# Softmax weights divided by their row sums on GpSimd, before their transposes

## The chip, the cores and the metric

The kernel runs on one core of a Trainium2 chip. The metric is the device time of one execution in microseconds (us). TensorE is called PE here (its weight loads PEld), VectorE DVE, ScalarE ACT, GpSimd POOL, and SyncE, which issues the DMAs, SP.

## The reference

Two layers of a hybrid decoder, 512 tokens of width 1024, each with five attention branches of four heads of 64, which are gated, projected and summed. The change concerns how a softmax branch divides by its sums:

```python
def _masked_softmax(logits, mask):
    l = jnp.where(mask, logits, -jnp.inf)
    m = jnp.max(l, axis=-1, keepdims=True)
    ...
    e = jnp.where(mask, jnp.exp(l - m), 0.0)
    return e / jnp.maximum(jnp.sum(e, axis=-1, keepdims=True), 1e-30)
```

A is DSA (a top-k mask from an indexer), B is FoX (a forget-gate bias), D is NSA (a sum of a compressed, a selected and a window part, each with a gate per head and token), E is attention into 256 memory tokens. C, stick breaking, has no softmax. Each branch output is multiplied with SiLU of its `z` projection before it is projected to width 1024.

## The kernel before

Activations lie transposed, channels on the partitions and 512 tokens along the row. Weights come in tiles of 128x1024 (`wload`, L281): each is split by ACT and DVE (L269, L270) into a high part `whi` and a rest `wlo`, so that a projection (`proj`, L503) is 3 x 8 matmuls of 128x512 into one PSUM bank `pj`.

An attention section is a Python generator, and `weave` (L652) interleaves its steps with those of generators that project: mem attention with `merge(2)`, the NSA projections and top-k (L1392); NSA attention with `merge(4)`, `dsa_proj` and the rest of top-k (L1393); DSA attention with `merge(3)` and `fox_proj` (L1394); FoX attention with `merge(0)` (L1395); then `merge(1, YB)` alone (L1396). `merge` needs the finished branch (`yhi`, `ylo`) that it projects. The tile framework sets the order of each engine at build time: it takes instructions in order of emission as far as their inputs and buffers are ready by its own cost estimates, weight loads earlier (`early`, L291). `after` (L191) pins a few orders by hand. At run time each engine keeps the order that it was given.

`causal` (L572) handles a causal softmax branch by blocks of 128 queries, i = 0 to 3, each with 128(i+1) keys, one head per step. A head: `qk` writes scores to a bank of tag `S` (two banks); `softmax_p` (L542) adds the mask and takes the row extreme on DVE (tile `P`, `nm`), then ACT takes the exponential with the sum of each row to `sums`. `finish`, called two heads later (lag 2), transposes `P` by 128x128 pieces on PE into a bank of tag `T` (three banks, tile `pt`), and evacuates it to `PT` on ACT or DVE in turn. After the fourth head `pv_pair` (L562) multiplies values with `PT` into a bank `Y` (channels on partitions, 128 queries along the row), and `done` follows. `P` has three buffers, shared by tag with two other tiles.

Queries lie along the row of `Y`, so the sums, one per query on its partition, do not fit it. `head_rows` (L611) takes the reciprocals `r` (`inv_sums`, L605), spreads each over 64 columns (`rb_`; on ACT at L616, or on DVE at L618 with the NSA gate), and transposes that in two pieces on PE (L621) into a bank `hr`. `gated_y` (L637) multiplies `hr` with `Z` to `g` (L640), then `Y` with `g` (L642), and `finish_y` splits `y` into `yhi` and `ylo`. NSA (L1180) does so for each of its two causal parts: `hr` copied to `rs_` (L1183), `Y` times `rs_` to `od` (L1185); the compressed part comes from two matmuls into a third bank `oc`; two adds (L1193, L1194) and the product with `Z` (L1196) end the block. `mem_attn` (L1259) works by pairs of heads, without a lag, its four heads of a block in one `Y`.

POOL only fills halves of key tiles with zeros (`k_stack`, L476).

## Time and profile before

| | |
|---|---|
| median of 3 runs | 1350.59 us (1350.27 to 1351.06) |
| the profiled execution, its own time | 1351.01 us |
| its span | 1349.2 us |
| PE busy | 1310.1 us (97%), 7240 matmuls |
| DVE busy | 892.8 us (66%) |
| ACT busy | 689.0 us (51%) |
| POOL busy | 11.4 us (1%) |

The span runs from the first to the last instruction that was recorded; the time of the execution has some 1.8 us more around it. Durations below are from that one execution. Recorded times of PE's neighbouring matmuls overlap, so where one ends against the next tells more than its duration. Waits are inferred from semaphores, and a wait is put down to what came last.

### The profile page before, as it was taken

How to read it: one execution, taken by the hardware profiler on the slowest of the kernel's cores; microseconds unless marked ns; L12 is line 12 of the kernel's file. 1: busy time of each engine (PE TensorE's matmuls, PEld its weight loads, DVE VectorE, ACT ScalarE, POOL GpSimd, SP SyncE). 2: the span in 40 equal slices, each digit the busy share in tenths (PEclk: the TensorE clock that was granted, in tenths of full speed). 3: DMA queues.
4: the chain of work that ended last, by engine and by line, in shares of the span. 5: the costliest groups of instructions: out<-in, count | busy, mean ns of one | idle time of the engine just before them, and what ended most of it. 6: DMA issues, size and time to landing. Idle time of an engine off the chain costs nothing.

```text
span 1349.2 us, 18962 instructions
## 1 busy us (share of the span) xinstructions
PE 1310.1 (97%) x7240; PEld 1068.4 (79%) x7240; DVE 892.8 (66%) x1847; ACT 689.0 (51%) x1300; POOL 11.4 (1%) x28
## 2 busy tenths in 40 slices
PE   7999999999999999999999999999999999999997
PEld 6777777878888788878887777777788778887896
DVE  6887999767655444545567799995676463454554
ACT  6887834357545434434447795534574452343340
POOL 0000000000000000000000000000000000000000
PEclk9999999999999999999999999999999999999998
DMA  6442321321123132224524313222122222323231
GB/s 215 139 127 77 110 78 63 94 78 59 63 79 102 55 94 78 71 84 130 183 81 126 109 63 110 85 68 84 57 69 63 86 86 66 100 77 103 94 111 63
DMA packets 40235, 124.11 MB, mean 92 GB/s; under 512 B 4432, under 2 KB 6480, under 8 KB 40144
## 3 DMA queue, kind: packets, MB, share of 16 engines
q1 hardware_dynamic: 40144, 122.89, 28.5%
q8 instruction: 57, 0.93, 0.3%
q14 instruction: 34, 0.28, 0.1%
HBM read 118.16 MB, written 4.72 MB: 91 GB/s over the span
## 4 chain that ended last, share of the span: by engine, by line
PE 70%; ACT 6%; DVE 5%; issue 2%; DVEq 0%; ACTq 0%
PE pj L259 58%; PE Y L259 3%; PE S L259 3%; PE pt L556 3%; ACT whi L269 2%; DVE wlo L270 1%; PE hr L621 1%; ACT sw L430 1%; ACT sw L431 1%; PE sbz L259 1%; DVE P L546 0%; ACT P L547 0%; DVE score L902 0%; DVE m L901 0%; ACT Qi L848 0%
## 5 line engine op out<-in xcount | busy, mean ns | idle before, releaser
L259 PE MATMUL pj<-h_hi,whi 128*128 128x512 f32 x1088 | 429.5, 396 | 0.7 <-DVE rt L433 0.7
L259 PE MATMUL pj<-h_hi,wlo 128*128 128x512 f32 x1088 | 429.0, 394 | 0.0
L259 PE MATMUL pj<-h_lo,whi 128*128 128x512 f32 x1088 | 429.0, 394 | 0.0
L270 DVE TENSOR_TENSOR wlo<-wraw,whi 128x1024 fp32r<-128x1024 f32 x183 | 223.7, 1223 | 228.1 <-ACT whi L269 217.0
L269 ACT ACTIVATE whi<-wraw 128x1024 fp32r<-128x1024 f32 x183 | 193.4, 1058 | 319.9 <-PE pj L259 213.9
L259 PEld LDWEIGHTS pj<-h_hi,wlo 128*128 128x128 f32 x1088 | 204.5, 188 | 42.8 <-DVE wlo L270 2.3
L259 PEld LDWEIGHTS pj<-h_hi,whi 128*128 128x128 f32 x1088 | 204.6, 188 | 40.5 <-issue 1.7
L259 PEld LDWEIGHTS pj<-h_lo,whi 128*128 128x128 f32 x1088 | 204.6, 188 | 40.4 <-issue 1.8
L547 ACT ACTIVATE P<-P,nm 128x128 f32<-128x128 f32 (+3 forms) x128 | 71.6, 559 | 67.7 <-DVE nm L546 64.2
L259 PE MATMUL pj<-yhi,whi 128*128 128x512 f32 (+1 forms) x192 | 71.9, 374 | 2.9 <-ACT yhi L269 2.9
L259 PE MATMUL pj<-yhi,wlo 128*128 128x512 f32 (+1 forms) x192 | 71.6, 373 | 0.0
L259 PE MATMUL pj<-ylo,whi 128*128 128x512 f32 (+1 forms) x192 | 71.5, 372 | 0.0
L556 PE MATMUL pt<-CA,P 128*128 128x128 f32 x384 | 62.7, 277 | 2.6 <-ACT P L1274 1.3
L546 DVE CUSTOM_DVE_ANT_0 P<-S,CA 128x128 f32<-128x128 f32 (+3 forms) x104 | 47.6, 468 | 18.1 <-PE S L259 18.0
L556 PEld LDWEIGHTS pt<-CA,P 128*128 128x128 f32 x384 | 44.9, 141 | 18.2 <-ACT P L1274 6.0
L259 PE MATMUL S<-Ks,Qs 128*128 128x256 f32 (+2 forms) x160 | 51.0, 358 | 6.6 <-DVE nm L546 6.5
L394 ACT ACTIVATE G<-pj 128x512 f32<-128x512 f32 x92 | 53.6, 582 | 0.3
L902 DVE MATCH_REPLACE8 score<-m,score 128x256 f32<-128x256 f32 (+2 forms) x96 | 51.7, 541 | 0.0
L901 DVE MAX8 m<-score 128x8 f32<-128x256 f32 (+2 forms) x96 | 49.7, 546 | 0.0
L799 DVE SCALAR_TENSOR_TENSOR G<-G,pj 128x512 f32<-128x512 f32 x64 | 43.6, 681 | 3.6 <-PE pj L259 3.3
L800 DVE TENSOR_TENSOR acc<-acc,G 128x512 f32<-128x512 f32 x64 | 44.0, 688 | 0.9
L259 PEld LDWEIGHTS pj<-yhi,whi 128*128 128x128 f32 x192 | 36.2, 188 | 10.4 <-ACT yhi L269 4.0
(478 smaller groups left out, 2006.1 us busy)
## 6 DMA issues: line engine op xcount, KB each, us to landing
wraw<-in_wall_dram SPq DMA_DIRECT2D x192, 512.0 KB, 3.7
wc<-in_wall_dram SPq DMA_DIRECT2D x16, 256.0 KB, 6.1
x<-in_xt_dram SPq DMA_DIRECT2D x8, 256.0 KB, 7.0
mraw<-in_memt_dram SPq DMA_DIRECT2D x4, 512.0 KB, 4.7
xo<-in_xt_dram SPq DMA_DIRECT2D x8, 256.0 KB, 4.3
xspill<-xn SPq DMA_DIRECT2D x8, 256.0 KB, 2.2
xo<-xspill SPq DMA_DIRECT2D x8, 256.0 KB, 4.0
out_dram<-o SPq DMA_DIRECT2D x8, 256.0 KB, 2.2
```

The source lines that it names most:

```text
L259: return nc.tensor.matmul(out_, lhsT, rhs, start=start, stop=stop, **kw)
L269: nc.scalar.activation(hi, raw, AF.Copy)
L270: nc.vector.tensor_sub(lo, raw, hi.bitcast(F32))
L394: i = nc.scalar.activation(*a, **k)
L430: nc.scalar.activation(sw[a], p[b], AF.Copy)
L546: nc.vector.tensor_tensor_reduce(P, S, mask, -1.0, 3e38, OP.add, OP.min, nm)
L547: nc.scalar.activation(P, P, AF.Exp, bias=nm, scale=-1.0, accum_out=sums)
L556: nc.tensor.transpose(pt[:, 128 * j:128 * j + 128], x[:, c:c + 128], ident)
L799: nc.vector.scalar_tensor_tensor(G, G, gc, p, op0=gop, op1=OP.mult)
L800: nc.vector.tensor_add(acc, acc, G)
L901: nc.vector.max(m8, lv.work[i])
L902: nc.vector.match_replace(lv.work[i], m8, lv.work[i], REPL)
```

## The change

After each second head of a part (in mem attention: after each pair), `inv_sums` is taken of the two heads' sums, in NSA multiplied with the two gates, and GpSimd multiplies each of the two `P` tiles, in place, with its column of it. The transposes then take the divided weights, so `head_rows` goes, with `hr`, `rb_`, `rs_`, `g` and `od`. In NSA the selected part, the window part and the compressed part (`rest`) all add up in one bank `Y`; the first matmul alone starts it. `gated_y` multiplies `Y` with `Z` directly. The lag of `causal` goes from two heads to three, mem attention gets a lag of one pair, and the tag of `P` has five buffers in place of three. `hold` keeps what `after_qk` did: a PV group comes after the scores issued last. In the diff, blank lines and longer runs of removed lines are left out (the functions before stand above):

```diff
@@ -541,7 +541,7 @@
     def softmax_p(S, n, mask, sums):
-        P = wk.tile([128, T], F32, name="P", tag="P", bufs=3)[:, :n]
+        P = wk.tile([128, T], F32, name="P", tag="P", bufs=5)[:, :n]
         nm = sm.tile([128, 1], F32, name="nm", bufs=6)
         nc.vector.tensor_tensor_reduce(P, S, mask, -1.0, 3e38, OP.add, OP.min, nm)
         nc.scalar.activation(P, P, AF.Exp, bias=nm, scale=-1.0, accum_out=sums)
...
@@ -559,46 +559,67 @@
         evac(o, pt[:, :128 * nblk])
         return o
-    def pv_pair(Y, pr, V, PTs, nblk, last):
-        after_qk = recent[-1] if last is None else None
+    def pv_pair(Y, pr, V, PTs, nblk, last, hold, first, end):
         for j in range(nblk):
             for e in (1, 0):
-                m = mm(Y[64 * e:64 * e + 64, pr], V(e, j), PTs[e][:, 128 * j:128 * j + 128], j == 0, j == nblk - 1)
-                after(m, last, after_qk)
-                last, after_qk = m, None
+                m = mm(Y[64 * e:64 * e + 64, pr], V(e, j), PTs[e][:, 128 * j:128 * j + 128], first and j == 0, end and j == nblk - 1,
+                       skip_group_check=True)
+                after(m, last, hold)
+                last, hold = m, None
         return last
     def causal(blocks, lag):
         pend = []
-        for i, scores, sums, mask, V, done in blocks:
+        for i, parts, rest, done in blocks:
             n = 128 * (i + 1)
-            st_ = {"P": [], "PT": []}
+            st_ = {"Y": None}
             share = (4, 2, 1, 1)[i]
...
+            for b, (scores, mask, V, gate) in enumerate(parts):
+                sums = sm.tile([128, 4], F32, name="sums", bufs=4)
+                Ps = []
+                pt_ = {"P": [], "PT": []}
+                for h in range(4):
+                    S = bank("S", "S")
+                    scores(h, S[:, :max(n, 256)], slice(128 * i, 128 * i + 128), slice(0, max(n, 256)))
+                    Ps.append(softmax_p(S[:, :n], n, mask, sums[:, h:h + 1]))
+                    if h % 2:
+                        r = inv_sums(sums[:, h - 1:h + 1], 2)
+                        if gate is not None:
+                            nc.vector.tensor_mul(r, r, gate[:, h - 1:h + 1])
+                        for e in range(2):
+                            x = Ps[h - 1 + e]
+                            nc.gpsimd.tensor_scalar(x, x, r[:, e:e + 1], None, op0=OP.mult)
+                    def finish(i=i, h=h, b=b, n=n, Ps=Ps, V=V, rest=rest, done=done, st_=st_, pt_=pt_, share=share, more=b + 1 < len(parts)):
+                        pt_["P"].append(Ps[h])
+                        if len(pt_["P"]) == share:
+                            PT = transposed(pt_["P"], share * (i + 1))
+                            pt_["PT"] += [PT[:, n * k:n * k + n] for k in range(share)]
+                            pt_["P"] = []
+                        if h == 3:
+                            if st_["Y"] is None:
+                                st_["Y"] = bank("Y", "T", (128, 2, 128))
+                            last = st_.get("last")
+                            hold = recent[-1]
+                            for pr in (1, 0):
+                                last = pv_pair(st_["Y"], pr, lambda e, j: V(2 * pr + e, j), pt_["PT"][2 * pr:], i + 1, last, hold,
+                                               b == 0 and pr == 1, not more and rest is None and pr == 0)
+                                hold = None
+                            st_["last"] = last
+                            if not more:
+                                if rest is not None:
+                                    rest(st_["Y"], last)
+                                done(st_["Y"])
+                    pend.append(finish)
+                    if len(pend) > lag:
+                        pend.pop(0)()
+                    yield
         for f in pend:
             f()
...
@@ -608,19 +629,6 @@
         nc.vector.reciprocal(r, r)
         return r
...
     def finish_y(y, i, Yhl):
         c = slice(128 * i, 128 * i + 128)
...
@@ -634,12 +642,9 @@
     def yt(name, bufs=2):
         return sm.tile([128, 2, 128], F32, name=name, bufs=bufs)
...
+    def gated_y(i, Y, Z, Yhl):
         y = yt("y")
-        nc.vector.tensor_mul(y, Y, g)
+        nc.vector.tensor_mul(y, Y, Z[:, :, 128 * i:128 * i + 128])
         finish_y(y, i, Yhl)
     xspill = dr.tile([128, KT, T], F32, name="xspill")
...
-                        R = wk.tile([128, T], F32, name="R", tag="P", bufs=3)[:, :n]
+                        R = wk.tile([128, T], F32, name="R", tag="P", bufs=5)[:, :n]
...
-                t = wk.tile([128, T], F32, name="sp_t", tag="P", bufs=3)[:, :w]
+                t = wk.tile([128, T], F32, name="sp_t", tag="P", bufs=5)[:, :w]
...
@@ -1045,10 +1050,9 @@
         def plain_attn(scores, mask, V, Z, Yhl):
             def blocks():
                 for i in range(NB):
-                    sums = sm.tile([128, 4], F32, name="sums", bufs=4)
-                    yield i, scores, sums, mask(i), V, lambda Y, i=i, sums=sums: gated_y(i, Y, inv_sums(sums, 4), Z, Yhl)
-            yield from causal(blocks(), 2)
+                    yield i, [(scores, mask(i), V, None)], None, lambda Y, i=i: gated_y(i, Y, Z, Yhl)
+            yield from causal(blocks(), 3)
         def dsa_attn():
             lv.YA = y_tiles()
...
@@ -1173,33 +1177,20 @@
             def blocks():
                 for i in range(NB):
...
+                    parts = [(lambda h, o, qs, ks, Kk=Kk: qk(o, lv.QD[h], Kk[0], Kk[1], qs, ks), MB[:, 384 - 128 * i:],
+                              lambda h, j, vo_=vo_: lv.VSW[:, 128 * j + vo_:128 * j + vo_ + 64], lv.gt[:, i, 4 + 4 * b:8 + 4 * b])
+                             for b, (Kk, vo_) in enumerate(((lv.KS, 0), (lv.KW, 64)))]
+                    def rest(Y, last, i=i):
+                        for pr in range(2):
+                            m = mm(Y[:, pr], lv.vcb[:, 128 * pr:128 * pr + 128], lv.PC[:, 128 * i:128 * i + 128], False, pr == 1,
+                                   skip_group_check=True)
+                            after(m, last)
+                            last = m
+                    yield i, parts, rest, lambda Y, i=i: gated_y(i, Y, lv.ZD[0], lv.YD)
+            yield from causal(blocks(), 3)
         def fox_proj():
...
@@ -1258,29 +1249,40 @@
         def mem_attn():
             lv.YE = y_tiles()
+            pend = []
             for i in range(NB):
-                sums = sm.tile([128, 4], F32, name="sumsE", bufs=3)
-                Y = None
+                st_ = {"last": None}
                 qs = slice(128 * i, 128 * i + 128)
-                last = None
                 for pr in range(2):
-                    P = wk.tile([128, T], F32, name="P", tag="P", bufs=3)
+                    sums = sm.tile([128, 2], F32, name="sumsE", bufs=3)
+                    P = wk.tile([128, T], F32, name="P", tag="P", bufs=5)
                     for e in range(2):
                         h = 2 * pr + e
                         S = bank("S", "S")[:, :NM]
                         qk(S, lv.QE[h], lv.KE[h], lv.KlE[h], qs, slice(0, NM))
                         nm = sm.tile([128, 1], F32, name="nm", bufs=6)
                         nc.vector.tensor_reduce(nm, S, AX.X, OP.max, negate=True)
...
+                        nc.scalar.activation(P[:, NM * e:NM * e + NM], S, AF.Exp, bias=nm, accum_out=sums[:, e:e + 1])
+                    r = inv_sums(sums, 2)
+                    for e in range(2):
+                        x = P[:, NM * e:NM * e + NM]
+                        nc.gpsimd.tensor_scalar(x, x, r[:, e:e + 1], None, op0=OP.mult)
+                    def finish(i=i, pr=pr, P=P, st_=st_):
+                        PT = transposed(P, 4)
+                        if pr == 0:
+                            st_["Y"] = bank("Y", "T", (128, 2, 128))
+                        st_["last"] = pv_pair(st_["Y"], pr, lambda e, j: lv.VE[:, j, 128 * pr + 64 * e:128 * pr + 64 * e + 64],
+                                              [PT[:, NM * e:NM * e + NM] for e in range(2)], 2, st_["last"], recent[-1], pr == 0, pr == 1)
+                        if pr:
+                            gated_y(i, st_["Y"], lv.ZE[0], lv.YE)
+                    pend.append(finish)
+                    if len(pend) > 1:
+                        pend.pop(0)()
+                    yield
+            for f in pend:
+                f()
         def out_proj():
```

## Rows read from the trace of the kernel before

**Rows 1.** The page, its first part: busy time of each engine, its share of the span and its instructions.

```profile
PE 1310.1 (97%) x7240; PEld 1068.4 (79%) x7240; DVE 892.8 (66%) x1847; ACT 689.0 (51%) x1300; POOL 11.4 (1%) x28
```

**Rows 2.** Waits of PE (its matmuls) over the whole span: engine, line and tile that waited, the engine and tile that released it; then us in total, number of waits, longest of them in us.

```profile
PE pj L259 <- ACT w L705: 9.8, 1, 9.8
PE S L259 <- DVE nm L546: 6.5, 11, 0.9
PE pj L259 <- ACT yhi L269: 2.9, 3, 1.3
...
PE pt L556 <- ACT P L1274: 1.3, 2, 0.6
```

**Rows 3.** Busy time of each engine in three stretches of layer 0 (us from the start of the span): top-k and mem attention; the end of NSA and DSA; FoX. Columns: length of the stretch, busy us (instructions) of PE, PEld, DVE, ACT, POOL, then the granted clock, the share of the DMA engines and GB/s.

```profile
155.00:250.00 95.00, 93.97 (x534) 73.49 (x531) 92.55 (x225) 42.28 (x85) 0.52 (x1) 1.00 0.29 92
...
385.00:455.00 70.00, 66.37 (x333) 53.64 (x332) 38.83 (x77) 37.69 (x74) 0.00 (x0) 1.00 0.26 83
455.00:580.00 125.00, 123.73 (x716) 102.88 (x715) 57.18 (x112) 46.47 (x87) 0.00 (x0) 1.00 0.24 76
```

**Rows 4.** Busy time of the transposes of L621 (`head_rows`) alone, over the span: us, then PE, PEld, granted clock, DMA.

```profile
0.00:1350.00 1350.00, 16.82 (x80) 8.97 (x80) 1.00 0.29 92
```

**Rows 5.** Timeline of PE around one pair of these transposes that stands between projections. Columns: start in us, duration in us of the group, engine, line, operation, tiles, shape, count.

```profile
228.07 0.39 PE L259 MATMUL pj<-h_hi,whi 128*128 128x512 f32 x1
...
228.75 0.39 PE L259 MATMUL pj<-h_hi,whi 128*128 128x512 f32 x1
228.99 0.38 PE L621 MATMUL hr<-CA,rb__2263 128*128 128x128 f32 x2
229.12 0.48 PE L259 MATMUL pj<-h_lo,whi 128*128 128x512 f32 x1
```

**Rows 6.** Timeline of PE around a pair that follows a PV group (`Y`); columns as above.

```profile
483.97 1.04 PE L259 MATMUL Y<-PT,VA 128*64 128x128 f32 x16
484.95 0.44 PE L621 MATMUL hr<-CA,rb__4764 128*128 128x128 f32 x2
485.14 0.47 PE L259 MATMUL pj<-h_hi,whi 128*128 128x512 f32 x1
```

**Rows 7.** Timeline of PE where a projection follows a PV group directly; columns as above.

```profile
167.35 0.66 PE L259 MATMUL Y<-PT,VE 128*64 128x128 f32 x8
167.94 0.50 PE L259 MATMUL pj<-h_hi,wlo 128*128 128x512 f32 x1
```

**Rows 8.** Groups of instructions on DVE, and one on ACT, that belong to the scaling of `Y`. Columns: line, engine, operation, tiles, shapes, count; busy us in all and mean ns of one; idle us before them and what ended it. Tiles with a number of their own stand once each: `rb__` on DVE and `od<-Y` are one of 16 each, `rb__` on ACT one of 24.

```profile
L640 DVE TENSOR_TENSOR g<-hr,Z 128x256 f32<-128x256 f32 x24 | 10.1, 422 | 24.8 <-PE hr L621 24.7
...
L608 DVE RECIPROCAL rsum<-rsum 128x4 f32<-128x4 f32 x40 | 6.9, 171 | 0.8
...
L607 DVE TENSOR_SCALAR rsum<-sums 128x4 f32<-128x4 f32 x32 | 5.3, 165 | 3.7 <-ACT P L547 3.6
...
L1193 DVE TENSOR_TENSOR od<-od 128x256 f32<-128x256 f32 x8 | 3.4, 424 | 0.2
...
L618 DVE TENSOR_TENSOR rb__9852<-rsum,gt 128x256 f32<-128x256 f32 x1 | 0.4, 428 | 0.0
...
L1185 DVE TENSOR_TENSOR od<-Y,rs__3167 128x256 f32<-128x256 f32 x1 | 0.4, 425 | 0.1
...
L616 ACT ACTIVATE rb__1751<-rsum 128x256 f32<-128x256 f32 x1 | 0.4, 418 | 0.6 <-DVE rsum L608 0.6
```

**Rows 9.** What POOL did. First its zero fills (L476) by tile: count, duration in ns as least, median, most, first and last start in us, shapes. Then from the timeline two of them, and the DVE subtractions that they overlap (start us, us, instruction, count). Last, all DVE subtractions of that line and tile over the span, with durations as in the first rows.

```profile
L476 POOL MEMSET Ks<- x16: 519/520/893, 12.3 to 958.7; 64x512 f32 x16
...
L476 POOL MEMSET KlE<- x8: 304/306/309, 57.1 to 704.0; 64x256 f32 x8
...
702.40 0.66 POOL L476 MEMSET KlE<- 64x256 f32 x2 [5.85 <-DVE h_lo L270]
...
701.65 1.89 DVE L270 TENSOR_TENSOR h_lo<-hr,h_hi 128x512 fp32r<-128x512 f32 x3
...
L270 DVE TENSOR_TENSOR h_lo<-hr,h_hi x16: 681/684/694, 36.1 to 706.2; 128x512 fp32r<-128x512 f32 x16
```

**Rows 10.** Timeline of the end of FoX attention in layer 0, the instructions around the last block. In brackets: idle time of the engine before it, and what ended it.

```profile
573.20 0.17 DVE L607 TENSOR_SCALAR rsum<-sums 128x4 f32<-128x4 f32 x1 [0.28 <-ACT P L547]
...
573.23 0.66 PE L556 MATMUL pt<-CA,P 128*128 128x128 f32 x4
573.41 0.18 DVE L608 RECIPROCAL rsum<-rsum 128x4 f32<-128x4 f32 x1
...
574.74 1.97 PE L259 MATMUL Y<-PT,VB 128*64 128x128 f32 x32
...
577.11 0.42 DVE L640 TENSOR_TENSOR g<-hr,Z 128x256 f32<-128x256 f32 x1 [3.53 <-PE hr L621]
...
577.57 0.42 DVE L642 TENSOR_TENSOR y<-Y,g 128x256 f32<-128x256 f32 x1
...
578.09 1.06 ACT L269 ACTIVATE whi<-wraw 128x1024 fp32r<-128x1024 f32 x1 [3.57 <-issue]
579.05 0.40 ACT L269 ACTIVATE yhi<-y 128x256 fp32r<-128x256 f32 x1
...
579.51 0.49 PE L259 MATMUL pj<-yhi,whi 128*128 128x512 f32 x1 [1.27 <-ACT yhi L269]
```

**Rows 11.** Waits of DVE, the row of the softmax's first pass (L546) on the transposes; columns as in rows 2.

```profile
DVE P L546 <- PE pt L556: 9.4, 3, 4.0
```

More of the change, by code (lines that the diff above doesn't have):

```diff
@@ L574, in causal @@
         pend = []
-        for i, scores, sums, mask, V, done in blocks:
+        for i, parts, rest, done in blocks:
             n = 128 * (i + 1)
-            st_ = {"P": [], "PT": []}
+            st_ = {"Y": None}
             share = (4, 2, 1, 1)[i]
-            for h in range(4):
-                S = bank("S", "S")
-                scores(h, S[:, :max(n, 256)], slice(128 * i, 128 * i + 128), slice(0, max(n, 256)))
-                P = softmax_p(S[:, :n], n, mask, sums[:, h:h + 1])
-                def finish(i=i, h=h, n=n, P=P, V=V, done=done, st_=st_, share=share):
-                    st_["P"].append(P)
-                    if len(st_["P"]) == share:
-                        PT = transposed(st_["P"], share * (i + 1))
-                        st_["PT"] += [PT[:, n * k:n * k + n] for k in range(share)]
-                        st_["P"] = []
-                    if h == 3:
-                        Y = bank("Y", "T", (128, 2, 128))
-                        last = None
-                        for pr in (1, 0):
-                            last = pv_pair(Y, pr, lambda e, j: V(2 * pr + e, j), st_["PT"][2 * pr:], i + 1, last)
-                        done(Y)
-                pend.append(finish)
-                if len(pend) > lag:
-                    pend.pop(0)()
-                yield
@@ L609, in inv_sums @@
         return r
-    def head_rows(r, gate=None):
-        rb_ = sm.tile([128, 4, 64], F32, name="rb_", bufs=1)
-        rr = r[:, :, None].to_broadcast([128, 4, 64])
-        if gate is None:
-            nc.scalar.activation(rb_, rr, AF.Copy)
-        else:
-            nc.vector.tensor_mul(rb_, rr, gate[:, :, None].to_broadcast([128, 4, 64]))
-        p = bank("hr", "T", (128, 2, 128))
-        for pr in range(2):
-            nc.tensor.transpose(p[:, pr], rb_[:, 2 * pr:2 * pr + 2].rearrange("p h d -> p (h d)"), ident)
-        return p
     def finish_y(y, i, Yhl):
@@ L1202, in nsa_attn @@
-            yield from causal(blocks(), 2)
+                    parts = [(lambda h, o, qs, ks, Kk=Kk: qk(o, lv.QD[h], Kk[0], Kk[1], qs, ks), MB[:, 384 - 128 * i:],
[7 more added lines that the diff above has]
+                            last = m
@@ L1273, in mem_attn @@
                         nc.vector.tensor_reduce(nm, S, AX.X, OP.max, negate=True)
-                        nc.scalar.activation(P[:, NM * e:NM * e + NM], S, AF.Exp, bias=nm, accum_out=sums[:, h:h + 1])
-                    PT = transposed(P, 4)
-                    if Y is None:
-                        Y = bank("Y", "T", (128, 2, 128))
-                    last = pv_pair(Y, pr, lambda e, j: lv.VE[:, j, 128 * pr + 64 * e:128 * pr + 64 * e + 64],
-                                   [PT[:, NM * e:NM * e + NM] for e in range(2)], 2, last)
-                    if pr == 0:
-                        yield
-                gated_y(i, Y, inv_sums(sums, 4), lv.ZE[0], lv.YE)
-                yield
+                        nc.scalar.activation(P[:, NM * e:NM * e + NM], S, AF.Exp, bias=nm, accum_out=sums[:, e:e + 1])
[17 more added lines that the diff above has]
+                f()
         def out_proj():
```

28 lines of the change are left out of this document (removed).

## The prediction

> **What bounds the kernel now.** I read the busy shares first: PE is busy 1310.1 of 1349.2 us, DVE 892.8, ACT 689.0, and POOL 11.4 [rows 1]. A busy PE could still be a waiting one, so the list of PE's waits comes second. PE waits 9.8 us once for the first weights, which no attention code touches, then 6.5 us in 11 pieces for score banks that the softmax's first DVE pass has to release (`nm`), then 2.9 us in three pieces for `yhi`, then 1.3 us for exponentials [rows 2]. So the end is set by the sum of PE's work, and the waits that an attention edit can move come to some ten microseconds. Third, the busy time by stretch: in the mem-attention stretch of layer 0 (155 to 250 us) DVE is at 92.55 of 95 us, nearly as full as PE; where the DSA section ends (385 to 455) PE loses 3.6 us of 70; in the FoX stretch (455 to 580) DVE is under half [rows 3]. The reader is to see that work taken from DVE or ACT earns nothing by itself, work taken from PE earns its pace, and DVE has no room to be delayed in just one kind of stretch, which occurs once in each layer.
>
> **Part 1: the `hr` transposes go from PE.** 40 calls of `head_rows` (8 NSA parts, 4 DSA, 4 FoX and 4 mem blocks, two layers) make 80 transposes, with 16.82 us of recorded busy time [rows 4]. Recorded times of neighbours overlap, so I price them by when the neighbours end. Plain projections follow each other every (228.75 - 228.07) / 3 = 0.227 us. With a pair of transposes between them, one ends at 229.14 and the next at 229.60: the pair costs 0.46 - 0.23 = 0.23 us [rows 5]. After a PV group (`Y`), the group ends at 485.01 and the projection behind the pair at 485.61, 0.60 us later [rows 6]. But a projection directly behind a PV group also ends late, 168.44 against 168.01, which is 0.43 us [rows 7]. Whatever follows a PV group pays for that switch, so removing the pair saves only 0.60 - 0.43 = 0.17 us there. 40 pairs at 0.17 to 0.23 give 6.8 to 9.2 us; I take 0.20, **-8.0 us**. The recorded 16.82 us would have promised twice that. The two compressed-branch matmuls per NSA block (`oc`) stay; they only write into `Y`.
>
> **Part 2: DVE and ACT.** Removed from DVE: 24 `g` products (10.1 us), 16 gate products at 0.43, 16 products `od` at 0.42, and 16 adds (`od`, two per NSA block) priced alike at 0.42: 10.1 + 6.9 + 6.7 + 6.7 = 30.4 us. Added: sums are inverted per pair of heads, so 80 calls in place of 40, 40 x (0.165 + 0.171) = 13.4 us, and 32 small gate products at about the same 0.165, 5.3 us: DVE is lighter by some 12 us. ACT loses 24 spreads of `rsum` at 0.42, and 16 copies `rs_` of the same shape [rows 8]. All of it lies beside PE's work, so it counts zero; if that cover were gone, as in the mem stretch, the mem part alone is 8 x 0.42 removed against 8 x 0.34 added, still nothing. The final product with `Z` stays, reading `Y` itself.
>
> **Part 3: 160 multiplications on GpSimd.** No row shows POOL reading a tensor. The nearest rows are its memsets: 0.306 us for 256 columns, and 0.52 us for 512, written on half the partitions [rows 9]. That is my lower end; a pass that reads as well as writes I bound at twice that, 1.04 us for 512 columns. DVE, over a tensor of 256 columns, takes 0.42 [rows 8], between the two, so I take 0.7 us for 512. For widths of 128, 256, 384 and 512 (32 heads each) the memset's slope gives 0.20, 0.31, 0.41 and 0.52: 46 us, and 32 mem heads of 256 make 10 more. So 56 us, at most 112, on an engine that is idle for 1338. POOL's other work, the zero fills of key tiles (`k_stack`), shares that queue: a fill that waits for its slot holds the multiplications behind it and these hold later fills. I count zero for it: by the stage weights a stretch of 125 us holds 16 FoX heads, about 8 us a head, two or three heads lie between a multiplication and its transposes, and it needs 1 or 2 us.
>
> The Trainium skill prices this directly: GPSIMD Engine Reference, section 3.1, gives an estimate of 1.8 cycles per element, 769 ns for 512 elements, and advises DVE for elementwise work. By that the sum would not move. No run here shows it yet.
>
> **Part 4: the wait that the change adds.** A transpose now waits for its pair's second exponential, two DVE operations and two multiplications. In mid-section the lag of three heads hides this. At the end of FoX nothing does: the pending heads are flushed, and `merge(1, YB)` needs the last block. In layer 0 `rsum` starts at 573.20 and ends at 573.59, the last head's transposes start at 573.23, the PV group ends at 576.71, `g` starts at 577.11, `y` ends at 577.99, `yhi` starts at 579.05 behind a weight conversion that ACT had taken at 578.09, and PE has by then stood still for 1.27 us [rows 10]. New: transposes start after rsum and two multiplications of 0.7 with handoffs of 0.1, about 575.2 instead of 573.23: +1.9 us (1.4 to 2.6). Given back: `g` and the way to it; from PV end to `y` it was 1.28 us, and one product with a handoff is 0.5 to 0.8: -0.5 to -0.8. Net +1.2 (0.6 to 2.1), on PE because it already waits there; in two layers **+2.4 us**. If ACT's conversion then falls differently against `yhi` up to 1 us a layer comes back, so the ends are +0.4 and +4.2. Queued behind the new wait are, on DVE, the reciprocal and whatever follows it (the next head's first pass), and on POOL the next pair.
>
> At the end of DSA, heads come in a bunch, and there DVE waited 9.4 us for transposes to free one of three `P` buffers [rows 11]. Five buffers relieve that; the multiplications lengthen the same loop. The two are of one size, so zero, with 2 us each way per layer. Elsewhere PSUM is easier (no `hr`, no `oc`, one `Y` per NSA block, though held through two parts), and waits for score banks should fall a little: **-1.0 us** (0 to -6.5, all of the second row of [rows 2]).
>
> **Part 5: does a multiplication hold DVE up?** POOL's fills at 702.40 ran inside DVE's subtractions of 701.65 to 703.54, which read two SBUF tensors, and none of the 16 of that group took over 0.694 us [rows 9]; a fill holds DVE by nothing. A multiplication also reads, and no row shows that, so its price lies between nothing and its whole length. It matters where DVE is full: 16 heads of mem attention a layer, 0.31 to 0.61 us each, 32 x that = 9.8 to 19.6 us, against 2 x 2.45 us of slack [rows 3]. I am nearest to the row: **+1.0 us**.
>
> A rule speaks against the change here. The Trainium skill, SBUF — State Buffer, "Who interferes with whom", says that a DVE instruction with two SBUF inputs contends with a GpSimd instruction that reads SBUF, not with one that only writes it, and that the later of them blocks completely. The fills above agree with its harmless half; the other half no run here shows. It would turn the case into the slower rival below.
>
> **Sum:** -8.0 + 2.4 - 1.0 + 1.0 = -5.6 us. The profiled execution took 1351.01 us (span 1349.2), 0.42 above the median of 1350.59, so 1351.0 - 5.6 - 0.4 = 1345.0 us.
>
> **The rivals.**
> (a) *GpSimd holds DVE up.* If each multiplication delays DVE by its length, the two mem stretches lose 9.8 - 4.9 = 5 to 19.6 - 4.9 = 15 us in place of my 1.0. That gives 1349 to 1359, say 1356. It decides from 10 us upward, about 0.34 us of delay for each of the 32 multiplications there (4.9 of slack, and 5.6 of gain to eat). For: DVE is at 97% there and wlo, which PE needs, stands in the same queue. Against: much of that stretch's DVE work is top-k, which nobody needs soon. The rule cited above is this rival; the traces so far show only fills, so 0.17.
> (b) *The new latency gives all of it back.* FoX ends at their dear end (4.2) and DSA bunches at theirs (4.0), no relief: -8.0 + 8.2 + 1.0, about 1351. For: PE already waits at just those places. Against: five buffers and the lag. 0.15.
> (c) *The relief is larger.* Score-bank waits vanish (-6.5), the `yhi` wait is met by other work (0.4), DVE is not held up: -8.0 - 6.5 + 0.4 = -14, 1336.5. For: `P` buffers and PSUM tiles stand behind several of PE's waits. Against: the score banks themselves stay two. 0.16.
> (d) My forecast, 1341 to 1348: 0.52.
>
> **How the numbers follow.** The range takes in (c) and most of (a): 1335 to 1357. About 0.2% (2.7 us) is what a measurement of this kernel can tell from no change. Faster than 1347.9: (c) and nearly all of the forecast, 0.65. Within: (b) with the edges of (a) and (d), 0.18. Slower than 1353.3: most of (a) and the bad end of (b), 0.17.
>
> **What would show it.** Right: no L621 group, PE's busy time down by up to 17 us while the time falls by much less; POOL near 56 to 112 us; PE's wait for `yhi` longer at both FoX ends; `wlo` still at 1.22 us. Rival (a): DVE operations with two SBUF inputs longer beside multiplications, and new PE waits for `wlo` between 155 and 250 us. Rival (b): PE waits on transposes (`pt`) released by POOL. Wrong altogether: POOL multiplications well over 1 us, or transposes that wait for POOL in the middle of sections.

## The result and the profile after

The changed kernel takes 1363.26 us (1361.86 to 1363.65, 4 runs) against 1350.43 us for the kernel before in the same runs: a ratio of 1.0096 [1.0078, 1.0113], 12.8 us slower. The forecast was 1345.0 us, with 1335 to 1357 as its range. The profiled execution took 1363.65 us, its span is 1361.8 us.

First the page's busy time, which answers to [rows 1], and the waits of PE, which answer to [rows 2] (us in total, number, longest).

```profile
PE 1308.5 (96%) x7160; PEld 1068.2 (78%) x7160; DVE 880.2 (65%) x1887; ACT 675.2 (50%) x1260; POOL 182.3 (13%) x188
```

```profile
PE pt L556 <- POOL P L596: 19.2, 29, 1.1
PE pj L259 <- ACT w L710: 8.9, 1, 8.9
PE S L259 <- DVE nm L546: 2.6, 5, 0.8
...
PE pj L259 <- ACT yhi L269: 2.0, 2, 1.0
```

The 80 transposes are gone (7240 to 7160 matmuls), and yet PE's busy time fell by only 1.6 us. DVE is lighter by 12.6 us, where Part 2 had said some 12, and ACT by 13.8. The waits for score banks fell from 6.5 to 2.6 us. A new row stands on top: 29 times the transposes of the weights waited for GpSimd, 19.2 us in all. The same row asked for by stretch shows where; the first is NSA of layer 0, the second DSA and FoX, the others the same in layer 1.

```profile
PE pt L556 <- POOL P L596: 5.4, 9, 0.9
PE pt L556 <- POOL P L596: 3.6, 5, 0.9
PE pt L556 <- POOL P L596: 5.6, 9, 0.9
PE pt L556 <- POOL P L596: 4.7, 6, 1.1
```

So 18 of the 29 waits, 11.0 us, lie in NSA, where the prediction had seen none. By the timeline, the last three heads of the two NSA sections, flushed right ahead of the last PV group, make six of these (4.4 us), and twelve (6.6 us) lie in mid-section. Seven more (4.4 us) lie in mid-section of DSA, in its third block, and four (3.8 us) at the ends of FoX. Mid-section is thus 19 waits with 11.0 of the 19.2 us. The mem heads (L1269) made none. The groups of POOL (line, engine, operation, tiles, shapes, count; busy us, mean ns; idle before and its releasers) show what one multiplication costs:

```profile
L596 POOL TENSOR_SCALAR P<-P,rsum 128x512 f32<-128x512 f32 x32 | 49.7, 1568 | 75.8 <-DVE rsum L593 42.0 <-DVE rsum L629 30.2 <-DVE nm L546 2.2
L596 POOL TENSOR_SCALAR P<-P,rsum 128x384 f32<-128x384 f32 x32 | 40.1, 1266 | 66.2 <-DVE rsum L593 25.7 <-DVE rsum L629 22.8 <-PE S L259 12.8
L1269 POOL TENSOR_SCALAR P<-P,rsum 128x256 f32<-128x256 f32 x32 | 31.4, 993 | 366.9 <-ACT Ks L486 216.8 <-DVE rsum L629 131.8 <-DVE score L910 18.0
...
L596 POOL TENSOR_SCALAR P<-P,rsum 128x128 f32<-128x128 f32 x32 | 18.9, 603 | 238.5 <-DVE rsum L629 173.6 <-DVE rsum L593 50.3 <-ACT P L547 13.1
```

From 128 to 512 columns the mean grows by (1568 - 603) / 384 = 2.5 ns a column, over a fixed part of 603 - 128 x 2.5 = 0.28 us.

**A wait in mid-section.** The timeline of NSA in layer 0, third block: on ACT the exponentials, on DVE the three steps from sums to factors, then POOL, then PE (start us, us, engine, line, operation, tiles, shapes, count; idle before and its releaser).

```profile
326.88 0.62 ACT L547 ACTIVATE P<-P,nm 128x384 f32<-128x384 f32 x1
...
327.62 0.17 DVE L628 TENSOR_SCALAR rsum<-sums 128x2 f32<-128x2 f32 x1
...
328.23 0.62 ACT L547 ACTIVATE P<-P,nm 128x384 f32<-128x384 f32 x1
...
328.84 0.15 DVE L629 RECIPROCAL rsum<-rsum 128x2 f32<-128x2 f32 x1
...
329.45 0.61 ACT L547 ACTIVATE P<-P,nm 128x384 f32<-128x384 f32 x1
...
329.50 0.15 DVE L593 TENSOR_TENSOR rsum<-rsum,gt 128x2 f32<-128x2 f32 x1
...
329.85 2.46 POOL L596 TENSOR_SCALAR P<-P,rsum 128x384 f32<-128x384 f32 x2 [3.67 <-DVE rsum L593]
...
331.18 0.51 PE L556 MATMUL pt<-CA,P 128*128 128x128 f32 x3
332.36 0.55 PE L556 MATMUL pt<-CA,P 128*128 128x128 f32 x3 [0.67 <-POOL P L596]
332.67 0.48 PE L259 MATMUL pj<-h_hi,wlo 128*128 128x512 f32 x1
```

Read upward from the wait: the second multiplication ends at 332.31, and the transposes that need it start at 332.36. The two multiplications start at 329.85, 0.2 us after the factors are done, and the way to the factors began at 327.62, when an exponential had just ended (326.88 + 0.62 = 327.50), the pair's second by the order of the code. From there to the second transposes it is 4.9 us: 2.35 until GpSimd starts, because the three short operations stand between other work in DVE's queue, and 2.46 on GpSimd. The exponentials come in a bunch, 1.2 to 1.4 us apart here, so three heads of lag are worth about 4 us at this place, not three times the 8 us that I had worked out as a mean. Behind the waiting transposes stand projections that have nothing to do with this head; PE takes its instructions in a fixed order, and 0.67 us is lost.

**A wait at a section's end.** The end of FoX in layer 0, to be read beside [rows 10]:

```profile
577.55 0.17 DVE L629 RECIPROCAL rsum<-rsum 128x2 f32<-128x2 f32 x1
...
577.91 3.11 POOL L596 TENSOR_SCALAR P<-P,rsum 128x512 f32<-128x512 f32 x2 [8.18 <-DVE rsum L629]
...
579.53 0.66 PE L556 MATMUL pt<-CA,P 128*128 128x128 f32 x4 [0.91 <-POOL P L596]
...
581.07 0.66 PE L556 MATMUL pt<-CA,P 128*128 128x128 f32 x4 [0.89 <-POOL P L596]
...
582.16 0.63 PE L259 MATMUL pj<-h_lo,whi 128*128 128x512 f32 x1
...
582.58 0.63 PE L259 MATMUL pj<-h_hi,wlo 128*128 128x512 f32 x1
...
583.14 2.99 PE L259 MATMUL Y<-PT,VB 128*64 128x128 f32 x32
...
587.11 0.50 PE L259 MATMUL pj<-yhi,whi 128*128 128x512 f32 x1 [0.98 <-ACT yhi L269]
```

The last pair's multiplications take 3.11 us, and PE stands still twice, 0.91 and 0.89 us. Then something follows that no row of before had at this place: two projections are 0.42 us apart instead of 0.227, and the PV group of 32 takes 2.99 us instead of 1.97 [rows 10]. The granted clock says what that is. By stretches of 25 us (length; busy us and instructions of PE, PEld, DVE, ACT, POOL; clock; DMA share; GB/s):

```profile
450.00:475.00 25.00, 22.43 (x141) 20.02 (x141) 10.04 (x23) 9.10 (x19) 9.30 (x7) 0.93 0.11 37
575.00:600.00 25.00, 22.23 (x117) 17.70 (x116) 10.44 (x18) 6.18 (x10) 3.11 (x2) 0.93 0.25 82
```

In the kernel before both stretches were granted 1.00. After the two waits PE ran for a while at 1.2 GHz instead of 2.4; the first row is the same after the three DSA waits of 449 to 455 us, which are 0.42 to 0.67 us long. Layer 1 has two such places again, behind its DSA waits and at its FoX end; none lies in NSA. Over the whole span the mean granted clock is 0.992 (before: 0.997), so I estimate the time lost to the lower level as (1 - 0.992) x 1361.8 = 10.9 us, against 0.003 x 1349.2 = 4.0 before. The 4.0 lie in the last 25 us of the span (granted 0.81 there), which the changed kernel has too; the difference is the four places.

### The profile page after: what moved, and what is told of

Read it like the earlier page. It is cut to its first block, busy times and chain, and to the rows that moved or that the text cites. A ratio compares the mean times of both kernels' runs of the same rounds, so it can differ in the third digit from the quotient of the medians.

```text
span 1361.8 us, 19167 instructions
## 1 busy us (share of the span) xinstructions
PE 1308.5 (96%) x7160; PEld 1068.2 (78%) x7160; DVE 880.2 (65%) x1887; ACT 675.2 (50%) x1260; POOL 182.3 (13%) x188
## 4 chain that ended last, share of the span: by engine, by line
PE 70%; ACT 11%; DVE 9%; issue 5%; POOL 3%; DMA 2%; POOLq 0%; SPq 0%; DVEq 0%; ACTq 0%
PE pj L259 60%; POOL P L596 3%; PE Y L259 3%; ACT whi L269 3%; PE S L259 2%; PE pt L556 2%; DVE wlo L270 1%; ACT sw L430 1%; ACT sw L431 1%; PE sbz L259 1%; ACT Qi L853 1%; ACT sp_t L388 1%; DMA wraw<-in_wall_dram 1%; DVE P L546 1%; DVE rt L433 1%
## 5 line engine op out<-in xcount | busy, mean ns | idle before, releaser
L270 DVE TENSOR_TENSOR wlo<-wraw,whi 128x1024 fp32r<-128x1024 f32 x183 | 223.8, 1223 | 234.6 <-ACT whi L269 223.8
L596 POOL TENSOR_SCALAR P<-P,rsum 128x128 f32<-128x128 f32 (+3 forms) x128 | 140.1, 1107 | 515.6 <-DVE rsum L629 292.4
L556 PE MATMUL pt<-CA,P 128*128 128x128 f32 x384 | 61.3, 278 | 20.6 <-POOL P L596 19.2
L1269 POOL TENSOR_SCALAR P<-P,rsum 128x256 f32<-128x256 f32 x32 | 31.4, 993 | 366.9 <-ACT Ks L486 216.8
L546 DVE CUSTOM_DVE_ANT_0 P<-S,CA 128x128 f32<-128x128 f32 (+3 forms) x104 | 47.9, 468 | 42.0 <-PE S L259 41.7
L259 PE MATMUL S<-Ks,Qs 128*128 128x256 f32 (+2 forms) x160 | 48.0, 353 | 2.7 <-DVE nm L546 2.6
L539 DVE COPY PT<-pt 128x512 f32<-128x512 f32 (+1 forms) x52 | 33.3, 643 | 21.5 <-PE pt L556 20.7
```

The lines of the kernel that those rows point to most:

```text
L259: return nc.tensor.matmul(out_, lhsT, rhs, start=start, stop=stop, **kw)
L270: nc.vector.tensor_sub(lo, raw, hi.bitcast(F32))
L539: nc.vector.tensor_copy(o, i)
L546: nc.vector.tensor_tensor_reduce(P, S, mask, -1.0, 3e38, OP.add, OP.min, nm)
L556: nc.tensor.transpose(pt[:, 128 * j:128 * j + 128], x[:, c:c + 128], ident)
L596: nc.gpsimd.tensor_scalar(x, x, r[:, e:e + 1], None, op0=OP.mult)
```

## The experiments

After the result I held theory T: *the weights come late*. A GpSimd multiplication is twice to three times as long as priced, PE's instructions stand in a fixed order, and work that is ready waits behind transposes that are not; without the multiplications the rest of the change is a gain. Rival R was rival (a) of the prediction: *GpSimd holds DVE up*, and everything that DVE feeds comes later. A further rival: *the other parts of the change*, the shared PSUM bank and the longer `P` rotation, cost the time. The line edited is mostly this one (L596, for the causal sections; L1269 is the same for mem attention):

```
nc.gpsimd.tensor_scalar(x, x, r[:, e:e + 1], None, op0=OP.mult)
```

Measured beside these runs, the kernel before took 1350.2 to 1350.7 us; ratios are to it.

| run | us | ratio |
|---|---|---|
| after (GpSimd) | 1363.26 | 1.0096 [1.0078, 1.0113] |
| e2_none, no multiplications | 1328.81 | 0.9841 [0.9827, 0.9854] |
| e4_side, GpSimd, nothing reads them | 1328.72 | 0.9841 [0.9827, 0.9854] |
| e3_lag2, none, lag 2, three `P` | 1337.15 | 0.9903 [0.9886, 0.9919] |
| e1_dve, all on DVE | 1336.06 | 0.9893 [0.9879, 0.9906] |
| e6_act, all on ACT | 1336.09 | 0.9895 [0.9880, 0.9910] |
| e9_mix, causal DVE, mem GpSimd | 1336.76 | 0.9899 [0.9884, 0.9914] |
| e11_split, one head ACT, one DVE | 1334.44 | 0.9885 [0.9872, 0.9899] |
| e14_half, each head half and half | 1347.07 | 0.9978 [0.9969, 0.9987] |
| e5_last, last block on DVE | 1349.15 | 0.9991 [0.9982, 0.9999] |
| e7_twice, GpSimd twice | 1433.28 | 1.0607 [1.0589, 1.0624] |
| e8_pin, GpSimd, order 1 | 1363.49 | 1.0100 [1.0085, 1.0115] |
| e10_hold, GpSimd, order 2 | 1350.35 | 1.0002 [0.9993, 1.0011] |

**The multiplications left out** (the division by the sums is not done):

```
-    nc.gpsimd.tensor_scalar(x, x, r[:, e:e + 1], None, op0=OP.mult)
+    pass
```

> The changed kernel without its 160 multiplications: the division by the sums (and the NSA gates) is left out, all else, lag, buffers, one bank, reciprocals, stays. Three theories. Late weights (T): the multiplication stands between exponential and transpose, 1.57 us for 512 columns where I had taken 0.7, PE waits for it 19.2 us in 29 pieces, and after four of these waits the clock is granted at half for 3.4 us. Held DVE (R): POOL's reads delay DVE, and PE through it. Rearrangement (B): lag, buffers and the one bank made a worse order by themselves. T and R: 1336 to 1343, below before by the 8 us of the transposes and some score-bank waits. B: 1352 or more.

Measured: 1328.81 us, below the low end of what I expected. Its busy row and its row of score-bank waits:

```profile
PE 1296.0 (98%) x7160; PEld 1065.0 (80%) x7160; DVE 873.2 (66%) x1887; ACT 674.0 (51%) x1260; POOL 11.0 (1%) x28
```

```profile
PE S L259 <- DVE nm L546: 3.5, 8, 0.8
```

So the change is two things of opposite sign: everything but the multiplications brings 21.5 us, the multiplications cost 34.5. The rival of the other parts falls.

**The multiplications on GpSimd, with a result that nothing reads** (division left out):

```
+    side = wk.tile([128, T], F32, name="side", tag="side", bufs=1)[:, :x.shape[1]]
-    nc.gpsimd.tensor_scalar(x, x, r[:, e:e + 1], None, op0=OP.mult)
+    nc.gpsimd.tensor_scalar(side, x, r[:, e:e + 1], None, op0=OP.mult)
```

> The multiplications stay on GpSimd, with the same reads and lengths, but write a scratch tile that nothing reads; the transposes take the undivided weights, so the division is left out of the result. T: as without multiplications, within 3 us of that run, no half clock in mid-kernel. R: most of the 13 us stays, 1352 to 1363. B: 1352 or more.

Measured: 1328.72 us, no difference from none at all. POOL is as busy as in the changed kernel, `wlo` on DVE takes 1223 ns on average as before, and DVE waited for POOL only where a `P` buffer was still being read. The page's busy row, the group of `wlo`, and the wait:

```profile
PE 1295.4 (98%) x7160; PEld 1063.2 (80%) x7160; DVE 879.1 (66%) x1887; ACT 674.2 (51%) x1260; POOL 184.4 (14%) x188
```

```profile
L270 DVE TENSOR_TENSOR wlo<-wraw,whi 128x1024 fp32r<-128x1024 f32 x183 | 223.7, 1223 | 228.3 <-ACT whi L269 217.6 <-PE pj L259 9.3
```

```profile
DVE P L546 <- POOL side L597: 1.9, 3, 1.0
```

The mean of `wlo` says little, since only 4 of its 183 ran at the same time as a multiplication. Where the two do meet, single operations are longer, on DVE (`rt`, which reads two tiles, up to 930 ns instead of 685) as on GpSimd (256 columns, up to 1431 ns instead of 926). Here are both as least, median and most, in ns:

```profile
L435 DVE TENSOR_TENSOR rt<-rt,sw x16: 674/685/930, 146.6 to 978.1; 128x512 f32<-128x512 f32 x16
```

```profile
L1271 POOL TENSOR_SCALAR side<-P,rsum x32: 923/926/1431, 159.4 to 897.4; 128x256 f32<-128x256 f32 x32
```

So the engines do hold each other up, but too seldom to matter: rival R falls as the cause, since 173 us of GpSimd work beside DVE cost no time that could be measured. What costs is that transposes need the result.

**The multiplications on DVE, on ACT, and the causal ones on DVE alone:**

```
-    nc.gpsimd.tensor_scalar(x, x, r[:, e:e + 1], None, op0=OP.mult)
+    nc.vector.tensor_scalar(x, x, r[:, e:e + 1], None, op0=OP.mult)        # e1_dve; e9_mix at L596 only
+    nc.scalar.activation(x, x, AF.Copy, scale=r[:, e:e + 1])               # e6_act
```

> The same multiplications on DVE in place of GpSimd, nothing else changed. T: DVE's pass over 512 columns is 0.74 us at most (as its passes with two inputs), so waits of the transposes fall from 19.2 us to under 5 and the clock stays whole: 1338 to 1346. R: also 1338 to 1346, unless the full stretch of mem attention shows; then 1347 to 1352. B: 1352 or more.

> The 128 multiplications of the causal sections on DVE, the 32 of mem attention on GpSimd. In the changed kernel no transpose of mem attention waited for POOL, and DVE is full there: 1333 to 1336.5, equal to or a little below all on DVE (1336.1). If GpSimd's reads hold DVE up where it is full, it is above: 1337 to 1342.

> All 160 multiplications on ACT (a copy with a scale per row). Its passes over 512 columns take about 0.72 us as its exponentials do, half of GpSimd's 1.57, so most waits of the transposes go, but each stands in the queue in which the weight conversions stand: 1336 to 1344. If only DVE's speed (0.48 us) were enough: 1345 to 1352.

Measured: 1336.06, 1336.76 and 1336.09 us; the first is 2 us below the range that I had given, the second just between its two ranges. The groups of 512 columns in e1_dve and in e6_act:

```profile
L596 DVE TENSOR_SCALAR P<-P,rsum 128x512 f32<-128x512 f32 x32 | 14.2, 483 | 0.4
```

```profile
L596 ACT ACTIVATE P<-P,rsum 128x512 f32<-128x512 f32 x32 | 21.1, 710 | 2.3 <-DVE rsum L629 1.9 <-DVE rsum L593 0.4
```

The same multiplication takes 0.48 us on DVE, 0.71 on ACT and 1.57 on GpSimd. DVE, busy for 923.0 us in e1_dve, and ACT, for 747.1 in e6_act, had the room; [rows 3] had made me fear for DVE in the mem stretch, and e9_mix, which keeps only that stretch off DVE, is no faster than e1_dve. The mem multiplications can stay on GpSimd at no cost that could be measured: no transpose waited for them.

**Only the last block of each causal section on DVE:**

```
+    (nc.vector if i == NB - 1 else nc.gpsimd).tensor_scalar(x, x, r[:, e:e + 1], None, op0=OP.mult)
```

> Only the last block (128 queries against 512 keys) of each causal section multiplies on DVE, all the others and mem attention on GpSimd. T: the section ends were the dear places, four halved clocks of 3.4 us and some 8 to 10 us of waits; these go, the waits inside NSA stay: 1347 to 1353. R: the multiplications in the full stretches of mem attention stay, so 1358 to 1363. B: 1358 to 1363.

Measured: 1349.15 us. The 32 heads of the last blocks, among them those flushed at a section's end, carry 14.1 of the 27.2 us between e1_dve and the changed kernel; the 96 causal heads of earlier blocks, with the mem heads, carry the other 13.1, and the waits that remain are theirs:

```profile
PE pt L556 <- POOL P L596: 11.0, 17, 1.2
```

All 17 are mid-section waits. I had expected the low clock to go with the last blocks; it went at the FoX ends, but stayed behind the DSA waits of both layers (rows by stretch, as above):

```profile
450.00:475.00 25.00, 24.64 (x149) 22.26 (x150) 10.26 (x20) 7.81 (x14) 0.31 (x1) 0.93 0.14 44
1100.00:1125.00 25.00, 21.71 (x146) 18.38 (x145) 12.64 (x39) 12.31 (x28) 4.93 (x4) 0.86 0.10 32
```

**Each multiplication followed by a second one on GpSimd, by 1.0:**

```
+    nc.gpsimd.tensor_scalar(x, x, 1.0, None, op0=OP.mult)
```

> The changed kernel with each multiplication on GpSimd followed by a second one of the same tile, by 1.0: twice the suspected cost. If each transpose is late by what the order did not allow for, every place pays again, mid-section too, and the 34.5 us between no multiplication (1328.8) and one (1363.3) come again about once: 1390 to 1410. If only the section ends pay, by two more multiplications each at four to six ends: 1373 to 1385.

Measured: 1433.28 us, 70.0 above the changed kernel, and above the end that I had given. Two waits of PE, and the clock of the span:

```profile
PE pt L556 <- POOL P L596: 53.7, 36, 3.2
...
PE pt L556 <- POOL P L1269: 6.8, 9, 1.6
```

```profile
core 0: 1431.5 us, clock 0.970
```

The waits grew by 53.7 + 6.8 - 19.2 = 41.3 us and the loss to the lower clock level by 0.030 x 1431.5 - 10.9 = 32.0 us: 73.3 us, against 69.7 by which the span grew (1431.5 - 1361.8). The second term is what I had not expected at this size. The mem transposes, which never waited for one operation a head, now wait for two.

**Order alone, first try:** the transposes are placed, in PE's order, behind the score group and the projection emitted last.

```
+    if j == 0:
+        after(m, recent[-1], recent_pj[-1])
```

> The changed kernel, multiplications on GpSimd, with one thing added: the transposes of a head are held on PE behind the scores and the projection emitted last, so they come later in PE's fixed order. If the lateness is one of place (the order puts a transpose where the weights would be ready if the multiplication were shorter, with projections standing behind it), the waits in mid-section, 11 of the 19 us, go, and the section ends stay: 1348 to 1356. If instead the multiplications are too slow as such for what flows through, it stays at 1360 to 1365.

Measured: 1363.49 us with 18.6 us of waits in 26 pieces. By the expectation's words this is the time of its other branch, multiplications too slow as such. But the edit did not test that: the waits in NSA, which it was to remove, stayed at 18 in 11.0 us, and where waits went, in the third block of DSA, others came at the ends of DSA. Since the transposes in NSA did not move away from their weights, the run decides nothing on place.

**Order alone, second try:** in blocks 2 and 3, where each head's transposes form a group of their own, they are ordered behind the newest exponential emitted so far, that is of a later head; the list of PE's waits shows no new wait for exponentials.

```
+    if j == 0 and recent_exp and isinstance(P, list) and len(P) == 1:
+        after(m, recent_exp[-1])
```

> The changed kernel, multiplications on GpSimd; the transposes of blocks 2 and 3 (384 and 512 keys) are ordered behind the newest exponential of the section, three heads on, which moves them later in the fixed order without any new wait on it at run time. The hold of the earlier run moved few of them and left the waits at 18.6 us. If place is what is wrong in mid-section, the waits of 11 us in NSA fall by more than half, the section ends stay: 1350 to 1358. If not: 1360 to 1366.

Measured: 1350.35 us, 12.9 below the changed kernel, with the same multiplications at the same length. A group of POOL, a wait of PE, and the clock of the span:

```profile
L599 POOL TENSOR_SCALAR P<-P,rsum 128x512 f32<-128x512 f32 x32 | 49.7, 1569 | 71.8 <-DVE rsum L596 20.3 <-ACT P L548 19.4 <-DVE rsum L632 16.1
```

```profile
PE pt L557 <- POOL P L599: 12.6, 21, 1.0
```

```profile
core 0: 1349.0 us, clock 0.996
```

The span fell by 12.8 us. PE's waits for POOL fell by 6.6 us, those for score banks rose by 2.4 (2.6 to 5.0), and its idle time fell by 5.2 in all; its busy time fell by 7.6, of which the clock's loss, from 10.9 to 0.004 x 1349.0 = 5.4, makes 5.5. By place, the waits fell in NSA from 11.0 to 7.0 us, less than the half that I had expected, and in DSA from 4.4 to 2.0. At the FoX ends they stayed, and yet the low clock is gone there:

```profile
575.87 0.66 PE L557 MATMUL pt<-CA,P 128*128 128x128 f32 x4 [0.99 <-POOL P L599]
577.41 0.66 PE L557 MATMUL pt<-CA,P 128*128 128x128 f32 x4 [0.88 <-POOL P L599]
```

```profile
575.00:600.00 25.00, 22.01 (x122) 17.89 (x123) 10.64 (x15) 7.43 (x11) 2.35 (x2) 1.00 0.17 52
```

GpSimd's length alone is thus not the cost; the place of the transposes in PE's order, too close behind it, is part of it. Place does not explain all: this run still stands 14.3 us above the multiplications on DVE.

**Without multiplications, but with a lag of two heads and three `P` buffers** (division left out), to price the longer rotation by itself:

```
-    P = wk.tile([128, T], F32, name="P", tag="P", bufs=5)[:, :n]      # all users of the tag
+    P = wk.tile([128, T], F32, name="P", tag="P", bufs=3)[:, :n]
-    yield from causal(blocks(), 3)
+    yield from causal(blocks(), 2)
```

> The run without multiplications (division left out, 1328.8), with the lag of causal sections back at two heads and the P tag at three buffers. If lag and buffers made the part of its gain that the transposes taken out don't explain (21.5 less 9 or 10 us): 1337 to 1341. If that part came from PSUM banks and shorter ends: 1327 to 1331.

Measured: 1337.15 us, 8.3 above e2_none. Between the two profiles PE's idle time grows by 5.1 us and its busy time by 3.1, with a mean clock of 0.994 against 0.997. The waits for score banks are back to almost [rows 2]:

```profile
PE S L259 <- DVE nm L546: 6.1, 9, 1.3
```

**Two ways to share the work:** first head of a pair on ACT and second on DVE; and each head's columns half on GpSimd, half on DVE.

```
+    (nc.vector.tensor_scalar(x, x, r[:, e:e + 1], None, op0=OP.mult) if e
+     else nc.scalar.activation(x, x, AF.Copy, scale=r[:, e:e + 1]))              # e11_split
+    w = x.shape[1] // 2                                                          # e14_half
+    nc.gpsimd.tensor_scalar(x[:, :w], x[:, :w], r[:, e:e + 1], None, op0=OP.mult)
+    nc.vector.tensor_scalar(x[:, w:], x[:, w:], r[:, e:e + 1], None, op0=OP.mult)
```

> No multiplication on GpSimd: of each pair the first head is multiplied on ACT, the second on DVE, side by side. Each alone gave 1336. If what is left to the floor of 1328.8 is the length of the pair (two passes of 0.48 or 0.71 in a row): 1331 to 1335. If it is the engines' added work: 1335 to 1338.

> Each multiplication is cut in two halves of its columns, the first on GpSimd (about 0.93 us for 256 of 512 columns, where the whole took 1.57), the second on DVE. The loss against no multiplication is 34.5 us at 1.57 and 7.3 at 0.48 (DVE) and 0.71 (ACT). If it follows the length: 1337 to 1346. If it is GpSimd's handoffs and not its length that cost: 1352 or more.

Measured: 1334.44 us for the split, the lowest time here of a kernel that computes all, 16 us below the kernel before: a pair's two multiplications can run side by side, on engines with room. Its interval overlaps those of one engine alone, so the last 1.6 us are not shown. The halves give 1347.07 us, 1 us above the range for a cost that follows the length, and well below the 1352 of the other; half the columns on GpSimd take more than half the time, 951 ns for 256 against 1568 for 512, as the fixed part above says, and 24 waits with 10.6 us remain:

```profile
L596 POOL TENSOR_SCALAR P<-P,rsum 128x256 f32<-128x256 f32 x32 | 30.1, 951 | 134.9 <-DVE rsum L593 46.9 <-ACT P L547 45.9 <-DVE rsum L629 39.3
```

```profile
PE pt L556 <- POOL P L596: 10.6, 24, 1.6
```

## Why the prediction was wrong

**The sign of the rest was right, its size too small.** Parts 1, 2 and the relief of Part 4 were -8.0, 0 and -1.0. Without the multiplications the kernel gains 21.5 us. PE's recorded busy time fell by 14.1 us (1310.1 to 1296.0; the 80 transposes had 16.82 recorded [rows 4]), and its idle time from 1349.2 - 1310.1 = 39.1 to 30.7 us, 8.4 less. e3_lag2 gives 8.3 us of the 21.5 to lag and buffers. I had put the buffers at zero and the score banks at 1.0 with 6.5 as the far end. 13.2 us are left for the transposes, the single bank and the shorter section ends; these were not separated, so whether a pair of transposes cost more than 0.20 us stays open. What rival (c) described came in part: without the multiplications the score-bank waits fall from 6.5 to 3.5 us and do not vanish, and the waits for `yhi` are gone; the whole gain is larger than its 14 us.

**The step that failed first is Part 3, the price of one multiplication.** I bounded it by 0.52 us (the fill) and 1.04 us (twice that) for 512 columns and took 0.7. It takes 1.57: the upper bound was a factor that I chose and no row, for an engine that no row of before showed reading anything. The Trainium skill's figure that I cited (GPSIMD Engine Reference, section 3.1) is given there as the best case of a loop, 769 ns measured for 512 elements, not as the price of this operation; it is half of what this trace shows. The same section's advice to use DVE for elementwise work agrees with e1_dve. The 56 us of POOL work were summed at the fill's price; at the 0.7 us that I took they would have been 56 x 0.7 / 0.52 = 75. They came out as 182.3 - 11.0 = 171.3.

**The second step that failed is the sentence in Part 4 that "in mid-section the lag of three heads hides this".** It rested on a mean of 8 us a head in FoX. Heads come in bunches, 1.2 to 1.4 us apart in the stretch shown, a first head waits for its pair's second, and the transposes' place in PE's order leaves a few us. 19 of the 29 waits lie in mid-section of NSA and DSA; with the last blocks off GpSimd, e5_last still stands 13.1 us above e1_dve; and e10_hold wins 12.9 us by order alone. The two steps hang together: in e6_act, where ACT multiplies in 0.71 us, about the price that I had taken, PE waits 0.8 us for the weights in all and the kernel takes 1336.09 us, so at that length the lag does cover nearly all. The ends of NSA, where heads are flushed as in FoX, had no price at all; PE waits 4.4 us there.

**The DSA bunch** was put at zero, with 2 us each way per layer. PE's waits there are 1.8 and 2.6 us, each followed by a stretch at the low clock, while DVE's wait for a `P` buffer [rows 11] fell only from 9.4 to 7.0. Part 4 had seen that heads come in a bunch here, and still took the mean for the rest.

**The end of FoX** was priced at +1.2 us a layer for the wait, 2.1 at most. The two waits there cost 1.8 us in layer 0, and `yhi` waits 0.98 in place of 1.27. That term was nearly right; the stretch at the low clock that followed it was missing from the sum. It need not follow: e10_hold has the same two waits without it.

**Sum of what the multiplications cost.** From e2_none to the changed kernel the span grows by 1361.8 - 1326.7 = 35.1 us. PE's idle time grows from 30.7 to 53.3, 22.6 us, of which 19.2 are the waits for POOL. Its busy time grows by 12.5 us: 10.9 - 4.0 = 6.9 by the clock. The last 5.6 us of busy time stay open. The terms come from one profile of each kernel; that the waits and the clock are the larger part of the cost is supported by e7_twice, where the same two terms add up to the change within 4 us, and by e10_hold, where idle time and clock make 10.7 of 12.8.

**Part 5 and rival (a)** are refuted by e4_side as far as the time goes: the +1.0 us should have been nothing. Rival (a)'s sign, DVE operations with two SBUF inputs that are longer beside multiplications, did come, without its cost: in the changed kernel `rt` at 330.05 us took 0.92 us instead of 0.69 behind the multiplication of 329.85, and one of 256 columns on GpSimd, behind the `wlo` of 323.57, took 1756 ns instead of 924. The rule of the Trainium skill (SBUF — State Buffer, "Who interferes with whom") on which rival (a) was checked would have made the case slower through DVE. The trace agrees that such operations contend, on either engine; the time came out slower, but not by that way. By the time alone, rival (a) with its 1349 to 1359 would have looked nearly right. **Rival (b)** named the true mechanism, PE waiting on transposes released by POOL, but only at the section ends, and at 1351. The prediction's last paragraph had "multiplications well over 1 us, or transposes that wait for POOL in the middle of sections" as what would make it wrong altogether; both came true.

What stays open: a lag of four heads was not tried; what the last 5.6 us of busy time are; and why the low clock follows some of these waits and not others.

## What to carry to other kernels

A slow idle engine was free here only for work whose consumer was not queued closely behind it: with the same GpSimd work the kernel took 1328.7 us when nothing read it, 1350.4 us when its readers stood further back and 1363.3 us when they stood close. Judge cover by the spacing of the nearest heads and by what stands behind the waiting instruction in the bound engine's order, not by a mean spacing over the stretch. And when no row shows an operation, let the range follow from that: ask what the result would be at three times the nearest row, which here was the truth.

## What the runs showed of the hardware

- GpSimd multiplied a float32 tile by one factor per partition in 0.28 us + 2.5 ns a column (603 ns for 128, 1568 for 512), DVE in 283 and 483 ns, ACT in 391 and 710.
- 160 such operations beside a DVE that is busy for 66% of the span cost no time (1328.72 against 1328.81 us). Single operations that met were longer: in e4_side `rt`, which reads two tiles, 930 ns instead of 685, and a multiplication of 256 columns 1431 ns instead of 926.
- In the changed kernel two waits of 0.9 us close together, with only four transposes between them, were followed by a stretch of PE at 1.2 GHz (matmuls 0.42 us apart instead of 0.227; clock 0.93 over 25 us, which is 1.75 us). In e10_hold waits of 0.99 and 0.88 us at the same place were not (clock 1.00). With waits up to 3.2 us (e7_twice) the mean clock fell to 0.970.
